# Instance norm over volumes on one core: chunk sums of a tile by one two-chunk VectorE instruction and one ScalarE instruction, last tile stored in two pieces

## Chip, cores, metric

One core of a Trainium2 chip. The metric is the device time in microseconds (us), median of several executions. Before the change it was 1247.06 us (three runs, 1246.88 to 1249.86). Each run has a state: "slow" if it lies over 1.5% above the fastest run of the same kernel, "unknown" if it is a single run, otherwise "fast".

## The reference

```python
x = np.random.randn(8, 64, 32, 64, 64).astype(np.float32)     # eps = 1e-5
mean = np.mean(x, axis=(2, 3, 4), keepdims=True)
var = np.var(x, axis=(2, 3, 4), keepdims=True)
return ((x - mean) / np.sqrt(var + eps)).astype(np.float32)
```

There are 512 instances of 131072 numbers: 268.4 MB to read once and to write once. The input is already close to mean 0 and variance 1. So a plain copy of it passes the comparison with the reference.

## The kernel before

A tile has 128 partitions x 12288 columns (6.29 MB) in three chunks of 4096 columns. 42 tiles go through four slots, after two parts of one chunk each. SyncE (SP) issues the loads, ScalarE (ACT) the stores. A load waits until the slot's last store has landed. For each tile VectorE (DVE) and ScalarE share the sums, small operations and a matmul combine them over the partitions of an instance, the two engines share the centred squares, and then scale and shift in place.

```python
    def tile_on_vector(eng, t, lane, c1, c3, c4, c16):
        for j, part in ((0, chunk[0]), (3, t[:, COLS - TURN :])):        # 4096 and 1536 columns
            eng.reduce_sum(out=column(a, SUMS, j), in_=part, axis=AXIS)._wait_ge(
                landed[lane], c16
            ).then_inc(summed[lane], 1)
        over_instance(...)          # small operations around a matmul: minus the mean per chunk
        # ... chunk 0: subtract the mean in place, sum of squares; over_instance again; 1/std; shift ...
        eng.tensor_scalar(out=chunk[0], ...).then_inc(done[lane], 1)     # scale
        eng.tensor_scalar(out=chunk[1], ...).then_inc(done[lane], 1)     # scale and shift

    def tile_on_scalar(eng, t, lane, c1, c3, c4, c16, dst):
        for j, part in ((1, chunk[1]), (2, chunk[2][:, : CHUNK - TURN])): # 4096 and 2560 columns
            eng.activation(..., func=Act.Identity, accum_out=column(a, SUMS, j))
        # ... squares of chunks 1 and 2, square root ...
        eng.activation(out=chunk[2], ...).then_inc(done[lane], 1)        # scale and shift
        eng.dma_start(out=dst, in_=t)._wait_ge(done[lane], c3).then_inc(stored[lane], 16)
```

## Time and profile before

| | before |
|---|---|
| span of the profiled run | 1245.2 us |
| VectorE / ScalarE busy | 811.6 / 757.7 us |
| moved by DMA | 536.9 MB, 431 GB/s over the span, 434 in the middle |
| from one landing to the next | 29.0 us |
| landing to store issue | 21.9 us |
| load / store, issue to landing | 39.9 / 54.2 us |

"Issue to landing" is the time from the instruction that issues a transfer to the semaphore that tells of its end. Both are longer than a tile's 29.0 us, because a load or store first stands in line behind its forerunner.

### The profile page before, as it was taken

The numbers are of one execution on the slowest core, as the hardware profiler recorded it, in microseconds if no ns is written. First come the engines' busy times: TensorE is split into PE (matmuls) and PEld (weight loads), VectorE is DVE, ScalarE is ACT, GpSimd is POOL, SyncE is SP. The second block draws the span as 40 slices with busy tenths as digits, with TensorE's granted clock in tenths as the row PEclk, the third lists the DMA queues.
The fourth block names the chain that finished last, engine by engine and source line by source line (L and its number), as shares of the span: only waits on it lengthen the run. The fifth ranks groups of instructions, "written<-read, shape, count | busy, mean of one in ns | idle before, by whom it ended". The sixth has DMA issues, their size and how long they took to land.

```text
span 1245.2 us, 1950 instructions
## 1 busy us (share of the span) xinstructions
PE 52.7 (4%) x176; PEld 44.1 (4%) x176; DVE 811.6 (65%) x724; ACT 757.7 (61%) x433; POOL 2.7 (0%) x15
## 2 busy tenths in 40 slices
PE   0000000000000000000000000000000000000000
PEld 0000000000000000000000000000000000000000
DVE  2887666666666666666666666666666666666663
ACT  5876555566666665665556665666566555566653
POOL 0000000000000000000000000000000000000000
DMA  9999999999999999999999999999999999999998
GB/s 396 429 430 434 444 433 429 431 429 441 439 433 431 429 429 444 436 429 433 431 433 442 434 431 431 429 434 444 433 431 431 429 442 437 431 433 429 429 444 368
DMA packets 12674, 536.89 MB, mean 431 GB/s; under 512 B 1408, under 2 KB 1408, under 8 KB 1408
## 3 DMA queue, kind: packets, MB, share of 16 engines
q1 hardware_dynamic: 6336, 268.44, 49.9%
q10 hardware_dynamic: 6336, 268.44, 49.8%
q14 instruction: 2, 0.02, 0.0%
HBM read 268.44 MB, written 268.44 MB: 431 GB/s over the span
## 4 chain that ended last, share of the span: by engine, by line
another core or an unknown queue 82%; DMA 9%; DVE 3%; ACT 2%; SPq 1%; issue 1%; PE 0%; ACTq 0%
DMA slot<-in_x_dram 6%; DMA out_dram<-slot 4%; ACT unused L220 2%; SPq L357 1%; DVE small L157 1%; DVE slot L200 1%; DVE slot L193 1%; ACT unused L213 0%; PE psum L250 0%; DVE small L137 0%; DVE small L125 0%; DVE small L131 0%; DVE small L143 0%; SPq L355 0%
## 5 line engine op out<-in xcount | busy, mean ns | idle before, releaser
L213 ACT ACTIVATE unused<-slot 128x4096 uint8<-128x4096 f32 x84 | 249.3, 2968 | 310.5 <-DMA slot<-in_x_dram 308.1
L157 DVE TENSOR_REDUCE small<-slot 128x1 f32<-128x4096 f32 x84 | 255.3, 3081 | 279.6 <-DMA slot<-in_x_dram 279.6
L220 ACT ACTIVATE unused<-slot,small 128x4096 uint8<-128x4096 f32 x84 | 310.8, 3701 | 65.3 <-DVE small L143 65.3
L171 DVE CUSTOM_DVE_ANT_0 unused<-slot 128x4096 uint8<-128x4096 f32 x42 | 185.9, 4426 | 1.4
L233 ACT ACTIVATE slot<-slot,small 128x4096 f32<-128x4096 f32 x42 | 159.7, 3802 | 18.5 <-DVE small L188 18.5
L200 DVE TENSOR_SCALAR slot<-slot,small 128x4096 f32<-128x4096 f32 x42 | 101.1, 2408 | 0.0
L164 DVE TENSOR_SCALAR slot<-slot,small 128x4096 f32<-128x4096 f32 x42 | 98.8, 2353 | 1.5
L250 PE MATMUL psum<-small,avg 128*128 128x12 f32 (+1 forms) x168 | 50.4, 375 | 1144.3 <-DVE small L125 1144.3
L193 DVE TENSOR_SCALAR slot<-slot,small 128x4096 f32<-128x4096 f32 x42 | 98.6, 2347 | 0.0
L250 PEld LDWEIGHTS psum<-small,avg 128*128 128x128 f32 x168 | 42.1, 311 | 1152.5 <-DVE small L125 1152.5
L131 DVE TENSOR_REDUCE small<-psum 128x3 f32<-128x12 f32 x84 | 14.2, 169 | 58.0 <-PE psum L250 58.0
L227 ACT ACTIVATE small<-small,eps_t 128x3 f32<-128x3 f32 x42 | 12.6, 299 | 62.6 <-DVE small L143 62.6
L125 DVE TENSOR_TENSOR small<-small,belongs 128x12 f32<-128x12 f32 x84 | 14.3, 170 | 31.9 <-ACT unused L220 29.5
L185 DVE RECIPROCAL small<-small 128x3 f32<-128x3 f32 x42 | 7.4, 176 | 15.4 <-ACT small L227 15.4
L137 DVE TENSOR_TENSOR small<-small,belongs 128x9 f32<-128x9 f32 x84 | 14.3, 170 | 2.9
L220 ACT ACTIVATION_READ_ACCUMULATOR unused<-slot,small 128x1 f32 x84 | 15.7, 186 | 0.0
L213 ACT ACTIVATION_READ_ACCUMULATOR unused<-slot 128x1 f32 x84 | 15.6, 186 | 0.0
L143 DVE TENSOR_REDUCE small<-small 128x3 f32<-128x9 f32 x84 | 13.6, 162 | 2.9
L263 DVE TENSOR_REDUCE small<-slot 128x1 f32<-128x2048 f32 x2 | 4.6, 2282 | 8.9 <-DMA slot<-in_x_dram 8.9
L289 ACT ACTIVATE unused<-slot,small 128x4096 uint8<-128x4096 f32 x2 | 7.4, 3707 | 2.0 <-DVE small L266 2.0
L286 ACT ACTIVATE unused<-slot 128x2048 uint8<-128x2048 f32 x2 | 3.8, 1910 | 7.1 <-DMA slot<-in_x_dram 6.6
L188 DVE TENSOR_TENSOR small<-small 128x3 f32<-128x3 f32 x42 | 6.8, 162 | 1.4
(26 smaller groups left out, 21.1 us busy)
## 6 DMA issues: line engine op xcount, KB each, us to landing
slot<-in_x_dram SPq DMA_DIRECT2D x42, 6144.0 KB, 39.9
out_dram<-slot ACTq DMA_DIRECT2D x42, 6144.0 KB, 54.2
slot<-in_x_dram SPq DMA_DIRECT2D x2, 2048.0 KB, 10.0
out_dram<-slot ACTq DMA_DIRECT2D x2, 2048.0 KB, 27.7
```

What stands on the lines that cost most here:

```text
L125: eng.tensor_tensor(out=block(a, by_both, n, m), in0=spread(a, at, m), in1=belongs[:, :, :m], op=Alu.mult,)._wait_ge(*wait).then_inc(steps ...
L131: eng.tensor_reduce(out=a[:, by_instance : by_instance + n], in_=p.rearrange("p (n m) -> p n m", m=m), axis=AXIS, op=Alu.add,)._wait_ge(st ...
L137: eng.tensor_tensor(out=block(a, by_chunk, n, n), in0=spread(a, by_instance, n), in1=belongs[:, :, :n].rearrange("p i c -> p c i"), op=Alu ...
L157: eng.reduce_sum(out=column(a, SUMS, j), in_=part, axis=AXIS)._wait_ge(landed[lane], c16).then_inc(summed[lane], 1)
L164: eng.tensor_scalar(out=chunk[0], in0=chunk[0], scalar1=column(a, MEANS, 0), scalar2=None, op0=Alu.add,)._wait_ge(centred[lane], c1).then_ ...
L171: eng.tensor_tensor_reduce(out=unused[2][:], in0=chunk[0], in1=chunk[0], scale=1.0, scalar=0.0, op0=Alu.mult, op1=Alu.add, accum_out=colum ...
L193: eng.tensor_scalar(out=chunk[0], in0=chunk[0], scalar1=column(a, SCALES, 0), scalar2=None, op0=Alu.mult,)._wait_ge(scaled[lane], c1).then ...
L200: eng.tensor_scalar(out=chunk[1], in0=chunk[1], scalar1=column(a, SCALES, 1), scalar2=column(a, SHIFTS, 1), op0=Alu.mult, op1=Alu.add,)._w ...
L213: eng.activation(out=unused[j - 1][:, : part.shape[1]], in_=part, func=Act.Identity, accum_out=column(a, SUMS, j),)._wait_ge(landed[lane], ...
L220: eng.activation(out=unused[j - 1][:], in_=chunk[j], func=Act.Square, bias=column(a, MEANS, j), accum_out=column(a, SQUARES, j),)._wait_ge ...
L233: eng.activation(out=chunk[2], in_=chunk[2], func=Act.Identity, scale=column(a, SCALES, 2), bias=column(a, SHIFTS, 2),)._wait_ge(shifted[l ...
L250: eng.matmul(out=p[:, col : col + THIRDS * m], lhsT=avg[PART][:], rhs=a[:, at + m : at + m + THIRDS * m], start=True, stop=True,)._wait_ge ...
```

## The change

It means to save instructions (one fewer of a tile's sums on each engine) and to start the last store earlier, while the older store still drains. Core of the diff:

```diff
-        for j, part in ((0, chunk[0]), (3, t[:, COLS - TURN :])):
-            eng.reduce_sum(out=column(a, SUMS, j), in_=part, axis=AXIS)...
+        for j, n, part in (
+            ((0, 1, chunk[0]), (3, 1, t[:, COLS - TURN :]))
+            if last
+            else ((0, 2, t[:, : 2 * CHUNK]),)
+        ):
+            eng.reduce_sum(out=a[:, SUMS + j : SUMS + j + n],
+                in_=part.rearrange("p (n f) -> p n f", n=n), axis=AXIS)...
 ...
-        for j, part in ((1, chunk[1]), (2, chunk[2][:, : CHUNK - TURN])):
+        for j, part in (
+            ((1, chunk[1]), (2, chunk[2][:, : CHUNK - TURN]))
+            if last
+            else ((2, chunk[2]),)
+        ):
 ...
+        at = 0
+        if last:
+            at = CHUNK
+            eng.dma_start(out=dst[:, :at], in_=chunk[0])._wait_ge(
+                done[lane], c3 - 2
+            ).then_inc(stored[lane], 16)
         eng.activation(out=chunk[2], ...)
-        eng.dma_start(out=dst, in_=t)._wait_ge(done[lane], c3).then_inc(
+        eng.dma_start(out=dst[:, at:], in_=t[:, at:])._wait_ge(done[lane], c3).then_inc(
```

The counts of the semaphores, the columns of the matmul (nine in place of twelve) and the last waits follow from this.

More of the change, by code (lines that the diff above doesn't have):

```diff
@@ L149, in over_instance, with tile_on_vector @@
         )._wait_ge(steps[3], c1).then_inc(steps[4], 1)
-    def tile_on_vector(eng, t, lane, c1, c3, c4, c16):
+    def tile_on_vector(eng, t, lane, c1, c2, c3, c16, last=False):
         a, p = small[lane], psum[lane]
         chunk = [t[:, i * CHUNK : (i + 1) * CHUNK] for i in range(THIRDS)]
-        for j, part in ((0, chunk[0]), (3, t[:, COLS - TURN :])):
-            eng.reduce_sum(out=column(a, SUMS, j), in_=part, axis=AXIS)._wait_ge(
-                landed[lane], c16
-            ).then_inc(summed[lane], 1)
+        m = 4 if last else 3
+        for j, n, part in (
[3 more added lines that the diff above has]
+        ):
+            eng.reduce_sum(
+                out=a[:, SUMS + j : SUMS + j + n],
+                in_=part.rearrange("p (n f) -> p n f", n=n),
+                axis=AXIS,
+            )._wait_ge(landed[lane], c16).then_inc(summed[lane], 1)
         over_instance(
-            eng, a, p[:, 0:12], SUMS, 4, MEANS, True, c1, (summed[lane], c4),
+            eng, a, p[:, 0 : 3 * m], SUMS, m, MEANS, True, c1,
+            (summed[lane], c2 + 2 if last else c2),
             (sorted_[lane], meaned[lane], joined[lane], picked[lane], centred[lane]),
@@ L207, in tile_on_vector, with tile_on_scalar @@
         )._wait_ge(shifted[lane], c1).then_inc(done[lane], 1)
-    def tile_on_scalar(eng, t, lane, c1, c3, c4, c16, dst):
+    def tile_on_scalar(eng, t, lane, c1, c2, c3, c16, dst, last=False):
         a = small[lane]
         chunk = [t[:, i * CHUNK : (i + 1) * CHUNK] for i in range(THIRDS)]
-        for j, part in ((1, chunk[1]), (2, chunk[2][:, : CHUNK - TURN])):
+        for j, part in (
[3 more added lines that the diff above has]
+        ):
             eng.activation(
@@ L239, in tile_on_scalar, with tile_on_tensor @@
         )._wait_ge(shifted[lane], c1).then_inc(done[lane], 1)
-        eng.dma_start(out=dst, in_=t)._wait_ge(done[lane], c3).then_inc(
+        eng.dma_start(out=dst[:, at:], in_=t[:, at:])._wait_ge(done[lane], c3).then_inc(
             stored[lane], 16
         )
-    def tile_on_tensor(eng, t, lane, c1, c3, c4, c16):
+    def tile_on_tensor(eng, t, lane, c1, c2, c3, c16, last=False):
         a, p = small[lane], psum[lane]
         for at, m, col, before, after in (
-            (SUMS, 4, 0, sorted_, meaned),
+            (SUMS, 4 if last else 3, 0, sorted_, meaned),
             (SQUARES, 3, 12, sorted2, varied),
@@ L329, in over_tiles @@
             ctx.enter_context(eng.register(f"{on_tile.__name__}_c{m}"))
-            for m in (1, 3, 4, 16)
+            for m in (1, 2, 3, 16)
         ]
-        for c, m in zip(counts, (1, 3, 4, 16)):
+        for c, m in zip(counts, (1, 2, 3, 16)):
             eng.reg_mov(c, m)
@@ L337, in over_tiles @@
                 on_tile(eng, slots[s][:], s, *counts, *more)
-            for c, m in zip(counts, (1, 3, 4, 16)):
+            for c, m in zip(counts, (1, 2, 3, 16)):
                 eng.reg_add(c, c, m)
@@ L342, in over_tiles @@
             more = (out_t[k],) if with_target else ()
-            on_tile(eng, slots[k % SLOTS][:], k % SLOTS, c, 3 * c, 4 * c, 16 * c, *more)
+            more += (k == n_tiles - 1,)
+            on_tile(eng, slots[k % SLOTS][:], k % SLOTS, c, 2 * c, 3 * c, 16 * c, *more)
     def load_all(eng):
@@ L364, in load_all @@
             ).then_inc(landed[k % SLOTS], 16)
-        for s in range(SLOTS):
-            eng.wait_ge(stored[s], 16 * len(range(s, n_tiles, SLOTS)))
+        for k in range(n_tiles - SLOTS, n_tiles):
+            uses = k // SLOTS + 1 + (k == n_tiles - 1)
+            eng.wait_ge(stored[k % SLOTS], 16 * uses)
     def set_up(eng):
```

## The prediction

> **What bounds the kernel now.** I read the page from the top, then the transfers, one tile in the middle, and the end.
>
> ```profile
> PE 52.7 (4%) x176; PEld 44.1 (4%) x176; DVE 811.6 (65%) x724; ACT 757.7 (61%) x433; POOL 2.7 (0%) x15
> DMA  9999999999999999999999999999999999999998
> HBM read 268.44 MB, written 268.44 MB: 431 GB/s over the span
> slot<-in_x_dram SPq DMA_DIRECT2D x42, 6144.0 KB, 39.9
> out_dram<-slot ACTq DMA_DIRECT2D x42, 6144.0 KB, 54.2
> ```
>
> The first line is busy time: VectorE (DVE) has a third of the span free, ScalarE (ACT) more. The DMA row is full in 39 slices of 40. Every byte is read once and written once, 536.9 MB, so the floor at the steady rate of 434 GB/s (the middle of the span) is 1237 us, and the span is 1245.2. The last two lines give 6 MB transfers with the median time from issue to landing. A tile comes every 29.0 us (two transfers of 6.29 MB at 434 GB/s), so a load stays 39.9 us because it stands in line for about 10.9, and a store 54.2 because it stands in line for about 25.2.
>
> The timeline of a tile in the middle gives the chain in which the change acts (start, duration):
>
> ```profile
> 567.50 3.62 ACT L213 ACTIVATE unused<-slot 128x4096 uint8<-128x4096 f32 x1 [7.88 <-DMA slot<-in_x_dram]
> 567.50 6.08 DVE L157 TENSOR_REDUCE small<-slot 128x1 f32<-128x4096 f32 x2 [7.13 <-DMA slot<-in_x_dram]
> 571.11 2.32 ACT L213 ACTIVATE unused<-slot 128x2560 uint8<-128x2560 f32 x1
> ...
> 589.39 0.34 ACTq L240 DMA_DIRECT2D out_dram<-slot  x1
> 596.50 3.62 ACT L213 ACTIVATE unused<-slot 128x4096 uint8<-128x4096 f32 x1 [7.89 <-DMA slot<-in_x_dram]
> ```
>
> From landing to store issue is 589.39 - 567.50 = 21.9 us, and VectorE then sits idle 7.1 us until the next tile lands. The compute chain is neither the throughput limit nor, thanks to the 25 us line before the stores, what the DMA waits for.
>
> The end, in order of time: last landing, last store, and what the DMA began in each window (last column GB/s):
>
> ```profile
> 1205.76 6.08 DVE L157 TENSOR_REDUCE small<-slot 128x1 f32<-128x4096 f32 x2 [7.19 <-DMA slot<-in_x_dram]
> ...
> 1222.95 2.35 DVE L193 TENSOR_SCALAR slot<-slot,small 128x4096 f32<-128x4096 f32 x1
> 1223.07 3.80 ACT L233 ACTIVATE slot<-slot,small 128x4096 f32<-128x4096 f32 x1 [0.44 <-DVE small L188]
> 1225.21 2.41 DVE L200 TENSOR_SCALAR slot<-slot,small 128x4096 f32<-128x4096 f32 x1
> 1227.65 0.35 ACTq L240 DMA_DIRECT2D out_dram<-slot  x1
> ```
>
> ```profile
> 1226.00:1228.00 2.00, 0.00 (x0) 0.00 (x0) 1.62 (x1) 0.87 (x1) 0.00 (x0) 1.00 0.12 49
> 1228.00:1230.00 2.00, 0.00 (x0) 0.00 (x0) 0.00 (x0) 0.00 (x0) 0.00 (x0) 1.00 0.92 393
> 1240.00:1242.00 2.00, 0.00 (x0) 0.00 (x0) 0.00 (x0) 0.00 (x0) 0.00 (x0) 1.00 0.91 393
> ```
>
> A packet counts in the window in which it starts. 49 GB/s for 2 us is 98 KB, two packets of 49152 bytes: so between 1226 and 1228 only two of the 16 DMA engines still start anything, and the others have run out. That hole looks like the gain of an earlier store. The packet records of the trace say more: 14 engines finish the store before the last between 1226.45 and 1227.56 and idle until 1228.51, when the last store's first packets start (0.86 us after its issue). The two slow engines work on to 1228.70 and 1228.93 and go into the last store without a pause. Eight packets of 1.815 us each are 14.5 us: the 14 end at about 1228.51 + 14.6 = 1243.1, the slowest at 1228.93 + 14.5 = 1243.43, which is the last packet of the trace.
>
> **What the Trainium skill says.** "DMA: Bandwidth & Descriptors", section Specifications, puts the ceiling of the 16 engines at 435 GB/s; the trace agrees with 434 in the steady stretch (one packet of 49152 bytes in 1.815 us is 27.1 GB/s per engine). The same page, "Issuing engines are not separate DMA queues", says that transfers issued from different engines run on the same 16 DMA engines and interleave; the queues of loads and stores take 49.9% and 49.8% of them. Its "Rules for kernel authors" ask for at least 1 MiB per DMA; the two pieces of the last store are 2 and 4 MiB. The 2 MB stores at the start move 16384 bytes in 0.611 us, so three small packets cost 1.833 against 1.815, no real loss. "VectorE: DVE Perf Modes", section on the perf-mode tier table, has only 1x for tensor_reduce; the trace agrees: 4420 ns for 4096 columns and 1743 for 1536, which is (4420 - 1743)/2560 = 1.046 ns per column and 137 ns fixed. The size of the next estimate comes from that slope.
>
> **The change part by part.**
>
> Steady tiles (41 of 42). *VectorE:* 4096 + 1536 columns in two instructions, 6.08 us from start to end, become 8192 columns in one: 137 + 8192 x 1.046 = 8.70 us. Busy per tile goes from 6.16 to 8.70, +2.54; 41 tiles, +104 us, so 811.6 becomes about 916. *ScalarE:* loses 2.32 + 0.19 (the accumulator read) = 2.5 us a tile, 103 in all: 757.7 becomes about 655. Its single sum ends at +3.7 us, so VectorE now ends the sums alone, 2.6 us later than before. *Matmul and small operations:* nine columns instead of twelve; 372 against 378 ns, nothing. Nothing else in the chain moves. Landing to store issue: 21.9 + 2.6 = 24.5 us, still under 29.0, and VectorE's idle time before a tile is 4.5 us instead of 7.1. On the end it costs nothing: the store gets in line 2.6 us later and stands 22.6 us instead of 25.2; issue to landing falls from 54.2 to about 51.6. The time it lands, hence the reload of the slot, stays where it was.
>
> Start. Here tiles 0 to 2 run back to back on VectorE (starts 30.55, 52.32, 74.56), so delays add up: store issues go from 52.43, 74.67 and 96.90 to about 55.0, 79.9 and 104.8; tile 3, landed at 102.56, starts at about 104.7. But the stores ahead of them land at 61.94, 91.43 and 120.42, so the line is still 6.9, 11.5 and 15.6 us deep. The store queue doesn't run dry.
>
> Last tile. Sums as before, so its chain is unchanged: landing 1205.76, chunk 0 done at about 1225.30. The first piece is issued then, 2.3 us earlier than the whole store was. ScalarE first issues (0.41 us until its next instruction), then does chunk 2 at about 1225.74 to 1229.54, behind VectorE's chunk 1 (1227.62). So the second piece goes out at about 1229.57, 1.9 us later than the whole store did, with its first packet possible at 1230.43. The first piece can start from 1226.19 and takes 8 x 0.611 = 4.9 us per engine: from 1226.45 to 1231.3 on the fast engines, so the second piece is there in time. Fast engines: 1231.3 + 9.7 = 1241.0, a gain of 2.0 us. Slowest engine: 1228.93 + 4.9 + 9.7 = 1243.5, where it was.
>
> Sum: 0 from steady state and start; at the end 0 if two engines lag by 2.3 us as in this trace, at most 2.0 if they don't. How far they lag I take for chance: the records have some 30 scattered load packets that took 0.1 to 0.4 us longer. I choose a gain of 0.3 us on the median, since the lag seen nearly covers the hole: 1247.06 - 0.3, rounded to 1246.8.
>
> **Rivals.**
>
> *The tail gains in full.* All engines in step at the end would make it 1247.06 - 2.0 = 1245.1. For it: the hole in 1226 to 1228 is real on 14 engines. Against it: the last packet of the trace belongs to an engine that never paused.
>
> *The longer chain gets onto the path.* With four slots, 39.9 + 21.9 + 54.2 = 116.0 = 4 x 29.0: the ring seems full, so one may fear 2.6 us more per turn, that is 0.65 us a tile and 27 us in all, 1274. Against it: 36 us of this turn are standing in line, and only the store's line shrinks. It would take over 25 us more in the chain, or over 7.1 on VectorE per tile, before the DMA starved.
>
> *VectorE reads the two-chunk pattern slower.* Were the reduction over a two-row pattern twice as slow (17.4 us), VectorE's turn would be 33 us instead of 29.0 and the kernel 13% slower, 1410. Against it: the chunks adjoin, the columns are dense, and the slope above holds between two sizes.
>
> **Range and chances.** Before had 1246.88, 1247.06 and 1249.86, so one run in three lay 2.9 us up. The low end takes the full tail gain (1245.0); the high end leaves room for a median that catches such a run: 1249.0. Two per cent is 25 us; the tail has no more than 2 to give and the DMA already fills the span, so faster gets 0.003. Slower needs one of the last two rivals: 0.012. Within 2%: 0.985.
>
> **What would show it.** Right: a two-column reduction of 8192 columns, 41 times, at about 8.7 us; VectorE near 916 busy, ScalarE near 655; store issue to landing near 51.6 and load still 39.9; last landing near 1205.7; two last store issues about 4.2 us apart; in the window of the old hole at least 14 engines starting packets; last packet within 0.3 us of 1243.4. Wrong: loads landing over 29.1 us apart, a load standing in line much less than 10.9 us (a starved load queue), a reduction over 10 us, or a second piece that finds the DMA idle. If the last packet comes at 1241 to 1242, the lag of the slow engines was no fixed trait, and the first rival holds.

## The result, and the profile after

After: 1247.91 us median of six runs (1246.45 to 1249.68); before, in the same rounds and the earlier ones, 1248.31 of six (1246.72 to 1252.91). The ratio is 0.9994 with a 95% interval of 0.9972 to 1.0015: the same. (Ratios are the mean time of one kernel's fast runs over that of the other's of the same rounds, so not quite the ratio of the medians quoted.)

The page of the changed kernel, the lines of busy time and of the transfers:

```profile
PE 52.4 (4%) x176; PEld 44.1 (4%) x176; DVE 917.8 (74%) x683; ACT 662.6 (53%) x351; POOL 2.7 (0%) x15
HBM read 268.44 MB, written 268.44 MB: 431 GB/s over the span
slot<-in_x_dram SPq DMA_DIRECT2D x42, 6144.0 KB, 39.9
out_dram<-slot ACTq DMA_DIRECT2D x41, 6144.0 KB, 51.6
```

VectorE is busy 106 us more and ScalarE 95 less, and of the transfers only one number moved: the same 431 GB/s, the load's 39.9 us unchanged, the store's time down from 54.2 to 51.6. That is where the longer chain was paid: in standing in line.

The timeline of the last two tiles, cut to the sums, the last scalings and the stores:

```profile
1176.52 8.69 DVE L164 TENSOR_REDUCE small<-slot 128x2 f32<-128x8192 f32 x1 [4.54 <-DMA slot<-in_x_dram]
...
1201.00 0.35 ACTq L261 DMA_DIRECT2D out_dram<-slot  x1
1205.53 3.62 ACT L228 ACTIVATE unused<-slot 128x4096 uint8<-128x4096 f32 x1 [5.31 <-DMA slot<-in_x_dram]
1205.53 6.08 DVE L164 TENSOR_REDUCE small<-slot 128x1 f32<-128x4096 f32 x2 [4.56 <-DMA slot<-in_x_dram]
...
1224.98 2.41 DVE L210 TENSOR_SCALAR slot<-slot,small 128x4096 f32<-128x4096 f32 x1
1225.09 0.35 ACTq L251 DMA_DIRECT2D out_dram<-slot  x1
1225.49 3.80 ACT L254 ACTIVATE slot<-slot,small 128x4096 f32<-128x4096 f32 x1 [3.10 <-DVE slot L203]
1229.32 0.34 ACTq L261 DMA_DIRECT2D out_dram<-slot  x1
```

The first piece goes out at 1225.09 in place of 1227.65. VectorE's wait for the next tile, in brackets, fell from 7.2 to 4.6 us. The windows of the end (last two columns: share of the DMA engines by packets that start there, and GB/s):

```profile
1226.00:1228.00 2.00, 0.00 (x0) 0.00 (x0) 1.39 (x1) 2.00 (x1) 0.00 (x0) 1.00 0.82 352
1240.00:1242.00 2.00, 0.00 (x0) 0.00 (x0) 0.00 (x0) 0.00 (x0) 0.00 (x0) 1.00 0.46 197
1242.00:1244.00 2.00, 0.00 (x0) 0.00 (x0) 0.00 (x0) 0.00 (x0) 0.00 (x0) 1.00 0.04 16
```

The hole before the last store is gone: 352 GB/s between 1226 and 1228 where there were 49. The packet records don't name the DMA engine; they are told apart by taking a packet to the engine whose last packet ended where it starts. Read so, 13 of the 16 engines now finish between 1241.0 and 1241.8, where all had finished between 1243.1 and 1243.4, and none pauses before the last store any more. Three finish later, and one of them begins a packet of 32 KB after 1242 (16 GB/s for 2 us) and ends at 1243.27. Before, the last packet ended at 1243.43. So 1.3 to 2.1 us were gained on 13 DMA engines and 0.16 us on the one that counts; the span went from 1245.2 to 1244.9.

### The profile page after: what moved, and what is told of

Its sections match the earlier page's. It is cut to its first block, busy times and chain, and to the rows that moved or that the text cites. A ratio compares the mean times of both kernels' runs of the same rounds, so it can differ in the third digit from the quotient of the medians.

```text
span 1244.9 us, 1828 instructions
## 1 busy us (share of the span) xinstructions
PE 52.4 (4%) x176; PEld 44.1 (4%) x176; DVE 917.8 (74%) x683; ACT 662.6 (53%) x351; POOL 2.7 (0%) x15
## 4 chain that ended last, share of the span: by engine, by line
another core or an unknown queue 80%; DMA 9%; DVE 4%; ACT 3%; SPq 1%; issue 1%; PE 0%; ACTq 0%
DMA slot<-in_x_dram 5%; DMA out_dram<-slot 4%; DVE small L164 3%; ACT unused L235 2%; SPq L379 1%; DVE slot L203 1%; DVE slot L210 1%; PE psum L271 0%; ACT slot L254 0%; DVE small L139 0%; DVE small L127 0%; DVE small L133 0%; DVE small L145 0%; ACT small L242 0%
## 5 line engine op out<-in xcount | busy, mean ns | idle before, releaser
L164 DVE TENSOR_REDUCE small<-slot 128x2 f32<-128x8192 f32 (+2 forms) x43 | 362.2, 8424 | 174.3 <-DMA slot<-in_x_dram 174.3
L228 ACT ACTIVATE unused<-slot 128x4096 uint8<-128x4096 f32 (+1 forms) x43 | 154.2, 3587 | 205.6 <-DMA slot<-in_x_dram 202.0
L271 PE MATMUL psum<-small,avg 128*128 128x9 f32 (+1 forms) x168 | 50.1, 372 | 1144.5 <-DVE small L127 1144.5
L133 DVE TENSOR_REDUCE small<-psum 128x3 f32<-128x9 f32 (+1 forms) x84 | 14.0, 167 | 57.8 <-PE psum L271 57.8
L127 DVE TENSOR_TENSOR small<-small,belongs 128x9 f32<-128x9 f32 (+1 forms) x84 | 14.1, 168 | 31.0 <-ACT unused L235 29.6
L284 DVE TENSOR_REDUCE small<-slot 128x1 f32<-128x2048 f32 x2 | 4.6, 2282 | 8.7 <-DMA slot<-in_x_dram 8.7
L228 ACT ACTIVATION_READ_ACCUMULATOR unused<-slot 128x1 f32 x43 | 8.0, 186 | 0.0
## 6 DMA issues: line engine op xcount, KB each, us to landing
slot<-in_x_dram SPq DMA_DIRECT2D x42, 6144.0 KB, 39.9
out_dram<-slot ACTq DMA_DIRECT2D x41, 6144.0 KB, 51.6
```

Source lines behind the costliest of these rows:

```text
L127: eng.tensor_tensor(out=block(a, by_both, n, m), in0=spread(a, at, m), in1=belongs[:, :, :m], op=Alu.mult,)._wait_ge(*wait).then_inc(steps ...
L133: eng.tensor_reduce(out=a[:, by_instance : by_instance + n], in_=p.rearrange("p (n m) -> p n m", m=m), axis=AXIS, op=Alu.add,)._wait_ge(st ...
L164: eng.reduce_sum(out=a[:, SUMS + j : SUMS + j + n], in_=part.rearrange("p (n f) -> p n f", n=n), axis=AXIS,)._wait_ge(landed[lane], c16).t ...
L228: eng.activation(out=unused[j - 1][:, : part.shape[1]], in_=part, func=Act.Identity, accum_out=column(a, SUMS, j),)._wait_ge(landed[lane], ...
L271: eng.matmul(out=p[:, col : col + THIRDS * m], lhsT=avg[PART][:], rhs=a[:, at + m : at + m + THIRDS * m], start=True, stop=True,)._wait_ge ...
```

## The experiments

There were twelve runs of ten kernels (e11 repeats e3, e12 repeats e9). My theory: the DMA is always fed, so neither part of the change can move the time, and the end is set by one or two DMA engines that have fallen behind the others.

### e1: the new sums, the last tile stored whole

```diff
-        if last:
+        if False:
             at = CHUNK
```
(and one store fewer in the last wait)

> The new chunk sums in all tiles but the last, the last tile stored whole. My theory (the DMA is always fed, and two late DMA engines end the program): time as before within 0.3 us in the profile, stores 51.6 us from issue to landing, and the hole before the last store is back: about 14 of 16 engines idle from about 1226.5 to 1228.5, last packet at about 1243.4. Rival A (the longer chain costs something that the split tail gives back): a span longer than before's 1245.2 by 1 us or more. Rival B (the fewer instructions gain by themselves): shorter by 1 us or more.

Measured: 1246.57 us median of five, before 1246.82 of eleven, ratio 1.0002 (0.9989 to 1.0015). The profiled run happened to be one of the longer ones, 1249.22 us, span 1247.5; three of the five took 1246.1 to 1246.6. The windows at its end:

```profile
1226.00:1228.00 2.00, 0.00 (x0) 0.00 (x0) 2.00 (x2) 2.00 (x1) 0.00 (x0) 1.00 0.17 74
1228.00:1230.00 2.00, 0.00 (x0) 0.00 (x0) 2.00 (x1) 1.30 (x1) 0.00 (x0) 1.00 0.06 25
1230.00:1232.00 2.00, 0.00 (x0) 0.00 (x0) 0.05 (x1) 0.00 (x0) 0.00 (x0) 1.00 0.92 393
```

Three packets start in the first window and one in the second: the hole is back, and wider. One engine alone was far behind: its last load packet ended at 1206.02, while most engines had ended theirs by 1201.7. A tile has landed only when all 16 engines have, so the last landing came at 1208.17 in place of 1205.5, its store began that much later, and the late engine ended last again, at 1245.90. The span that was expected, 1245.2, was missed by this run for that cause; rival A would need the median to be longer, and it isn't. This is also what the longer runs of about 1249 us are, in the one that has a profile.

### e2: the old sums, the last store split

```diff
+        at = 0
+        if last:
+            at = CHUNK
+            eng.dma_start(out=dst[:, :at], in_=chunk[0])._wait_ge(done[lane], c3 - 2)...
```

> The sums of before in all tiles, only the last store split. My theory: the hole between 1226 and 1228 is filled as in the changed kernel, most engines end about 2 us earlier (1241 to 1242), the last packet stays at 1243 to 1243.5 and the span at 1245.0 within 0.3. Rival (the split gains its 2 us and the longer chain took them back): span about 1243.

Measured: 1246.85 us median of five (1246.76 to 1247.02), ratio 1.0000 (0.9987 to 1.0013); span 1245.1, last packet 1243.36. The windows:

```profile
1226.00:1228.00 2.00, 0.00 (x0) 0.00 (x0) 1.49 (x1) 2.00 (x1) 0.00 (x0) 1.00 0.82 352
1242.00:1244.00 2.00, 0.00 (x0) 0.00 (x0) 0.00 (x0) 0.00 (x0) 0.00 (x0) 1.00 0.04 16
```

The hole is filled and again a lone packet starts after 1242. So the split alone gains nothing either, and the longer chain had nothing to take back. The rival (span 1243) falls.

### e3 and e11: the copy without arithmetic, twice

```diff
-    over_tiles(nc.vector, part_on_vector, tile_on_vector)
...
-    over_tiles(nc.tensor, part_on_tensor, tile_on_tensor)
-    over_tiles(nc.scalar, part_on_scalar, tile_on_scalar, with_target=True)
+    over_tiles(nc.scalar, store_part, store_tile, with_target=True)   # store on landed
```

> Wrong result on purpose: no arithmetic at all, each tile is stored as soon as it has landed, by the same transfers in the same slots. It measures what the transfers alone take. My theory: the compute is hidden altogether, so span 1243 to 1245 and ratio 0.998 to 1.000; the two late engines are there without any compute. Rival (compute costs the DMA something, by SBUF contention or by waits): ratio under 0.995, that is over 6 us less.

> The copy without compute once more, to see whether its even finish repeats: if compute is what makes engines late, again no packet over 1.83 us after the first 100 us and all engines done within 0.8 us of each other at about 1241.5. If late engines are chance, this run may show one.

Measured: e3 1247.66 us median of six (1245.0 to 1252.14), ratio 1.0017 (1.0005 to 1.0029), just above the 0.998 to 1.000 expected. Its page shows no compute and the DMA at the full rate:

```profile
POOL 2.7 (0%) x15
HBM read 268.44 MB, written 268.44 MB: 432 GB/s over the span
```

Without any compute the kernel is no faster, which is the main result: there is no compute left to save. (The copy moves the same bytes, but its transfers stand otherwise to each other: in its trace a load lands 5.0 us after a store, before the change 10.9.) Its profiled run was the shortest of all, span 1243.3, and in it no engine was late: all 16 ended within 0.8 us, the last at 1241.75. So the part of the theory that expected late engines here was wrong, and for a while I took compute for their cause. e11, the same kernel once more, took 1251.48 us (span 1249.8, one run, state unknown). The windows of its end:

```profile
1238.00:1240.00 2.00, 0.00 (x0) 1.00 0.91 393
1240.00:1242.00 2.00, 0.00 (x0) 1.00 0.23 98
1242.00:1244.00 2.00, 0.00 (x0) 1.00 0.17 74
1244.00:1246.00 2.00, 0.00 (x0) 1.00 0.11 49
1246.00:1248.00 2.00, 0.00 (x0) 1.00 0.06 25
```

Four, three, two, one packets per window: most engines are done by about 1242, three stragglers go on, and the last ends at 1248.22. No compute engine ran. So late DMA engines can come without compute; how late they are differs from run to run of the copy (0.5 us behind most others in e3, over 6 in e11) and moves the time by more than the change could. Whether compute makes them more frequent is not shown. What stretches their packets is outside what these traces show.

### e4: all three sums on VectorE

```diff
-            else ((0, 2, t[:, : 2 * CHUNK]),)
+            else ((0, 3, t),)
...
-            else ((2, chunk[2]),)          # ScalarE
+            else ()
```
(and the count of sums that VectorE waits for)

> The changed kernel with all three chunk sums in one VectorE instruction (12288 columns, about 13.0 us, 4.3 more than two chunks) and none on ScalarE, last tile as in the change. VectorE's turn goes from 24.4 to 28.7 us, just under the 29.0 us that a tile's transfers take. My theory (only the turn of the busiest engine against 29.0 counts, the longer chain comes off the time a store stands in line): same time, span within 0.7 us of 1244.9, stores about 47 us from issue to landing in the middle, VectorE over 1090 us busy. Rival (every us on the chain counts when the four slots are full): 4.3 / 4 us a tile, 45 us in all, ratio about 1.036.

Measured: 1247.0 us median of four, ratio 0.9999 (0.9980 to 1.0017), span 1245.2. The costliest group by line (count, busy us, mean ns, idle before it) and the stores:

```profile
L164 DVE TENSOR_REDUCE small<-slot 128x3 f32<-128x12288 f32 (+2 forms) x43 | 536.9, 12488 | 2.5 <-DMA slot<-in_x_dram 2.5
```

```profile
out_dram<-slot ACTq DMA_DIRECT2D x41, 6144.0 KB, 40.4
```

VectorE waits for data 2.5 us in the whole run, against 280 in the kernel before, and still the time is the same. The stores stand in line less, 40.4 us to landing over all (I had put "about 47 in the middle"; it grows from 33 us after the start to 48 before the end, because VectorE catches up only 0.4 us a tile). VectorE was busy 1089.9 us. So the sums could grow by another 4.3 us a tile without anything to show. The rival (1.036) falls.

### e5: the two-chunk sum done twice

```diff
+            if not last:
+                eng.reduce_sum(out=a[:, 68:70],           # nobody reads it
+                    in_=part.rearrange("p (n f) -> p n f", n=n), axis=AXIS)...
             eng.reduce_sum(
```

> The changed kernel with the two-chunk sum done twice (the first into columns that nobody reads; the result stays right). VectorE's turn becomes 24.4 + 8.7 = 33.1 us, over the 29.0 of the transfers. My theory: VectorE is now the bound; 30.4 us to the first start, 41 turns of 33.1, then the last tile's 19.5 to its first piece and about 15 of transfer: span about 1423, ratio about 1.142; VectorE over 95% busy. Rival (8.7 us of latency fit into the 22.6 us that a store stands in line, so nothing happens): ratio 1.00.

Measured: 1420.72 us median of four, ratio 1.1384 (1.1365 to 1.1403); span 1419.1 against 1423 expected. Now both transfers take only about their own time:

```profile
slot<-in_x_dram SPq DMA_DIRECT2D x42, 6144.0 KB, 31.0
out_dram<-slot ACTq DMA_DIRECT2D x41, 6144.0 KB, 31.6
```

The turn of VectorE was 33.0 us (store issues at 162.44 and 195.40, for one) and the end followed it. Over 95% busy was not met, 1266.9 us are 89%, since VectorE waits within each tile for ScalarE and the matmul. With e4 this brackets the limit: 28.6 us a tile cost nothing, 33.0 cost 14%; the kernel before is at 22.2, the changed one at 24.4, where the tiles follow each other without a pause.

### e6, e7, e8: fewer slots

```diff
-    SLOTS = 4
+    SLOTS = 3          # e6, e8; 2 in e7
-    ROUNDS = n_tiles // SLOTS
+    ROUNDS = (n_tiles - 1) // SLOTS      # e6, e7, so that the last tile is treated as such
```

e6 and e7 are the changed kernel, e8 the one before.

> The changed kernel with three tile buffers in place of four. My theory (10.9 us of a load's and 22.5 us of a store's time is standing in line): a turn of three tiles is 87 us, load 29.0 + chain 24.5 + store 29.0 = 82.5, so 4.5 us are left for handovers and it just fits: ratio 1.000 to 1.012, load plus store about 62 us from issue to landing in place of 91.5. Rival (the ring of four slots is full because it is needed): 39.9 + 24.5 + 51.6 = 116 us over three tiles, 38.7 a tile, ratio about 1.33.

> The changed kernel with two tile buffers: here the chain must come onto the path. While one tile computes (24.5 us) the other one stores and loads (29.0 us at full rate), and each store-to-load handover on the same slot leaves the DMA idle for about 1.8 us (landing 0.4, next first packet 0.9, and the issue). My theory: about 30.8 us a tile, ratio about 1.06 (1.04 to 1.10), holes visible in the DMA row. Rival (buffers don't matter as long as the turn of VectorE is under 29.0): ratio 1.00.

> The kernel before (sums in two pieces on each engine, whole stores) with three tile buffers. With three buffers the changed kernel ran at 30.2 us a tile (its landings repeat every 90.7 us over three tiles) and its chain was on the path. My theory: the chain that is 2.6 us shorter now shows: 88.1 us over three tiles, 29.4 a tile, about 35 us less in all than the changed kernel with three buffers, as far as the transfers let it: ratio to before 1.000 to 1.012. Rival (handovers between transfers alone cost the 2.4%, the chain's length is still hidden): ratio 1.024 as there.

Measured: e6 1278.2 us (ratio 1.0241, 1.0224 to 1.0258), e7 1440.48 (1.1546, 1.1520 to 1.1571), e8 1277.62 (1.0256, 1.0218 to 1.0294; its four runs spread from 1265.0 to 1283.9). All three are slower than I expected, though far from the rival's 1.33 for e6. The windows from 300 to 900 us, of e6, e7 and e8 in this order:

```profile
300.00:900.00 600.00, 25.02 (x84) 21.02 (x84) 443.93 (x332) 313.57 (x164) 0.00 (x0) 1.00 1.00 423
```

```profile
300.00:900.00 600.00, 21.50 (x72) 18.05 (x72) 391.19 (x288) 275.45 (x144) 0.00 (x0) 1.00 0.92 379
```

```profile
300.00:900.00 600.00, 25.16 (x84) 21.04 (x84) 397.48 (x357) 365.76 (x208) 0.00 (x0) 1.00 1.00 434
1230.00:1264.00 34.00, 1.20 (x4) 1.00 (x4) 13.27 (x16) 11.75 (x8) 0.00 (x0) 1.00 0.54 234
```

In e8's profiled run the middle has the full 434 GB/s, 29.0 us a tile: the chain of before, 21.9 us, just fits three slots, as expected. The run is the fastest of the four, 1265.0, and what it lost lies at the start (landings up to 35.8 us apart until it settled) and at the end: with one slot fewer there is less of a store still in line when the last tile computes, so the DMA runs at 234 GB/s for the last 34 us, where the kernel before has 374. I had priced neither. The three longer runs have no profile. In e6 the chain of 24.5 us does not fit and the middle runs at 423 GB/s, 29.8 us a tile (the 30.2 us in the text of e8 come from one turn of the three slots). So at three slots the change's 2.6 us show in the middle of these two traces, while the times of the two kernels are not told apart.

e6 and e7 also show a cost that my sums left out. The DMA share of e6 is 1.00, yet it moves 423, not 434. In the packet records a load that doesn't stand in line starts slowly. After the first 100 us, where the first packet came within 1.3 us of the issue, the first 16 packets, one for each engine, took 2.59 us on average in e7 (39 loads), 2.63 in e5 (34) and 2.43 in e6 (10), in place of 1.815. It is not enough that no other load is under way: 12 such loads of e6 stood in line behind a store, and their first packets took 1.85. In e5, where a store joins at once, the second and third packets of each engine are long too (2.27 and 2.32), and in e7 the sixth and seventh (2.18 and 2.06), when a store joins. Stores themselves did this less (e7: 1.89, then 1.82). With four slots a load stands in line for 10.9 us, and its packets took 1.82 in the kernels before and after, so they never pay it. Why a load starts slowly is not shown.

### e9, e12, e10: copy with the work of one engine

```diff
+        eng.reduce_sum(..., in_=t[:, : 2 * CHUNK].rearrange("p (n f) -> p n f", n=2))   # e9, e12: VectorE
+        for c in chunks(t): eng.tensor_scalar(out=c, in0=c, scalar1=1.0, ..., op0=Alu.mult)
+        # e10: ScalarE: three sums, then Act.Identity on each chunk in place
```

> Wrong arithmetic on purpose: copy through the slots with VectorE work alone on each tile (the two-chunk sum, then a multiplication by 1 of each chunk), ScalarE only issues stores. It asks what makes single DMA engines late. Without compute all 16 ended within 0.8 us of each other; with the full compute the last one was 1.3 to 2.3 us behind the bulk. Theory V (VectorE's accesses to the slots delay some packets): last engine over 1 us behind the bulk, scattered load packets over 1.83 us in the middle of the run. Theory S (it is ScalarE's): none, and the last packet at 1241.0 to 1241.8.

> Wrong arithmetic on purpose: copy with ScalarE work alone on each tile (three sums, then an identity over each chunk), no VectorE work. Theory S (ScalarE's accesses delay some packets): last engine over 1 us behind the bulk, scattered long load packets. Theory V: none, last packet at 1241.0 to 1241.8. If both this and the VectorE copy show late engines, either kind of compute is enough; if neither does, it takes both, or chance.

> The copy with VectorE work alone once more, timed. Its single run took 1444.8 us, with transfer packets of 2.04 (loads) and 2.11 us (stores) on average in place of 1.815, stretched while VectorE worked and while it did nothing alike. Theory 1 (something outside the program slowed the transfers of that one run): all or nearly all runs now 1246 to 1253, packets at 1.815. Theory 2 (VectorE's work without ScalarE's, or the order of transfers that it makes, slows the transfers): again about 1440 in all runs.

Measured: e10 1251.13 us (one run, state unknown), one engine over 5 us behind the median of the 16 from about the ninth tile on. e9 1444.83 (one run, state unknown). e12, the same kernel as e9, timed: 1445.41, 1411.25, 1405.58, 1405.85, 1406.33; ratio of its fast runs 1.1289 (1.1266 to 1.1312). The profiled run of e12 was the slow one and is compared with nothing; e9's, alike, is in no better state. What both show, e9 here in the window from 300 to 900 us:

```profile
300.00:900.00 600.00, 267.55 (x71) 0.00 (x0) 1.00 0.98 372
```

Theory V and theory S both made compute the cause, and e11 shows that late engines need none. And a new question came up that I could not settle. The DMA is 98% busy and moves 372 GB/s, because its packets took 2.03 (loads) and 2.11 us (stores) on average; VectorE is not the bound (the window has it 268 of 600 us busy) and the packets are long while it idles too (2.01 and 2.10). All five runs of e12 took over 1405 us, so theory 1, something outside in one run, falls; the 1440 of theory 2 came once, the other four took 1405.6 to 1411.3 and have no profile. In both traces a load and a store land about 0.2 us apart, so both streams may go through the same partitions of their tiles at the same time, while in the kernel before a load lands 10.9 us after a store. In e9 the packets of the first two full loads, which land at 34.9 and 53.2 with no full store beside them, took 1.815 us, for the second while VectorE worked; the long ones begin with the next tile, the first whose load lands together with a store (86.5 us). That the streams then hinder each other in the memory would fit; no run tests it, and e8, at 3.6 us, is at full speed in its middle. It stays open. It bears on the change in one way: where load and store stand to each other was left as it was, at 10.9 us.

## Why the prediction was right

**Size and path of the new sums.** Predicted 8.70 us for 8192 columns from a straight line through two sizes; measured 8685 ns. The rate holds at this size too, 1.06 ns a column, so the rival of a slow two-row pattern fell. (That the slope "holds between two sizes" was no test, since any two points lie on a line; a third size, 2048 columns in 2282 ns, stood in the same lines.) VectorE 916 predicted, 917.8 measured. ScalarE was put at 655 and came to 662.6: the 95.1 us that went are 41 sums of 2.32 us. The reads of the accumulator (0.19 us), priced in as well, lie nearly all beside other work, so taking 41 of them away took no busy time.

**Off the path.** The step that carried the prediction was that a longer chain shortens only the store's line. Store 51.6 us to landing, as predicted; load 39.9, last landing 1205.51, unchanged. e4 and e5 show the limit on both sides: 6.4 us more a tile on VectorE than before cost nothing and 10.8 cost 14%, which agrees with the 7.1 us of the prediction. That it is the fourth slot that pays for the longer chain is likely from the middles of e6 and e8 (423 against 434 GB/s), but their times don't tell it.

**Start.** Store issues of about 55.0, 79.9 and 104.8 were predicted and came at 54.94, 79.29 and 103.66. The steps are 24.4 and not 24.9 us, since before the change the sums of these tiles were ended by ScalarE, 0.5 us after VectorE. It cost nothing either way.

**Tail.** "A gain of 2.0 us" on the fast engines, none on the slowest: measured 1241.0 to 1241.8 on 13 engines and 1243.27 for the last packet, against 1243.5 predicted. All 16 engines start packets in the window of the old hole (at least 14 predicted), the issues lie 4.23 us apart (4.2 predicted), and the second piece found the first still running. "How far they lag I take for chance" is not shown for this kernel. In the copy the lag did differ between two runs (e3, e11). But the last packets of the four profiled runs of about 1246.8 us with all the compute ended at 1243.43 (before), 1243.27 (after), 1243.36 (e2) and 1243.41 (e4), so there much the same lag came back each time; why is open. The sign that the prediction named for chance, a last packet at 1241 to 1242, did not come. What I had not seen is its reach: in e1 the late engine also delayed the landing of the last tile, so lag adds at two places, and it is as large as the 3 us between the shorter and the longer runs.

**Size.** The median was put at 1246.8 and came at 1247.91: three of the six runs were longer ones of 1249.1 to 1249.7, where one in three had been reckoned, and with one more of them it would have come at about 1249. That it lies between the two kinds of runs is luck, and tells nothing of the change. A gain of 0.3 us was put on it; against before, the span of the profiled run is shorter by 0.3, the median of the change by 0.4 and of e1 by 0.25, while that of e2 is longer by 0.03. None of these is told from zero by the times, whose intervals are 0.1 to 0.2% wide on each side. The rivals of a longer ring (1274, ratio 1.022) and of the slow pattern (1410) are outside the interval. The full tail gain of 2.0 us (ratio 0.9984) is not outside that of the whole change (0.9972 to 1.0015); against it speak the last packet at 1243.27, the five runs of e2, none below 1246.76 where the full gain would be about 1245, and, barely, the interval of e2 (0.9987 to 1.0013).

## What to carry to other kernels

When the DMA row is full, read from each transfer how long it stands in line before it moves: that is what a longer chain could eat here at no cost. It ends where the turn of the busiest engine reaches the transfers' time (here between 28.6 us a tile, which was free, and 33.0, which was not), or at the buffers. Before a hole in the DMA at the end is priced, look at which engines have it: the kernel ends with its last engine, and a hole on 14 of 16 was worth nothing here. A copy through the same buffers, run several times (here 1245.0 to 1252.1 us), tells whether there is any compute left to save.

## What the Trainium skill lacked or had wrong

- "DMA: Bandwidth & Descriptors" gives 435 GB/s as the ceiling of the fabric behind the 16 engines and says, under why a DMA increments its semaphore by 16, that the engines of a DMA finish independently. It lacks how far they drift apart in a program like this (for two of the engines it has the word "slower", without a figure): at the end of the copy the last engine was 0.5 us behind most others in one run (e3) and over 6 in another (e11), and the copy took 1245.0 to 1252.1 us.
- The same page lacks that a load which doesn't stand in line begins slowly: first packets of 49152 bytes in 2.4 to 2.6 us in place of 1.815 (e5, e6, e7). Its first-byte latency for the sync and scalar path, about 0.6 us in Specifications, compares with 0.86 us here from the start of a 0.35 us issue to the first packet of the last store, or 0.51 from the end of the issue.
- No page that I read has the state of e9 and e12: transfers at 372 GB/s, at 98% busy, in a program whose compute fits (VectorE 268 of 600 us busy). "Perfetto Trace Analysis", section Identifying the Most-Contended Engine, rightly advises judging DMA by bytes moved and not by occupancy; this is a case of it.
